# Attention values gathered over half a head from one ring of transposed probabilities

## The chip, the cores and the metric

The kernel runs on one core of one Trainium2 chip. The metric is the device time of one execution in microseconds (us); the time of a kernel is the median over its runs. TensorE (PE) multiplies matrices, VectorE (DVE), ScalarE (ACT) and GpSimd (POOL) do the elementwise work, and SyncE (SP) issues most DMAs. Each engine takes its instructions in a fixed order.

## What is computed

One block of a diffusion model: neighbourhood attention and a convolutional feed-forward network, each with a normalisation, a modulation and a residual. Cut to what matters here:

```python
SEQ, D_MODEL, NA_HEADS, CTX_LEN = 1024, 1024, 16, 256      # head dimension 64
q, k = rms_norm(split_heads(h @ w_q), q_gain), rms_norm(split_heads(h @ w_k), k_gain)
v = split_heads(h @ w_v)                                   # kc, vc: the same of the 256 context rows
# of each query: a window of 8 x 16 keys of the 16 x 64 grid, and all 256 context keys
s = jnp.concatenate([s_loc, s_ctx], axis=-1)
p = jax.nn.softmax(s.astype(jnp.float32), axis=-1)
y = (p_loc @ v_win + p_ctx @ v_ctx) @ w_o                  # per head, then all heads together
x = x + g1 * y
x = x + g2 * conv_ffn(modulate(rms_norm(x, norm2), sh2, sc2))
```

## The kernel before

**Numbers.** Everything is fp32, but most matmuls are done in the faster float32r type on operands split in two: a high half (a ScalarE copy that rounds) and a low half (the rest, a subtraction on VectorE or GpSimd). A product is then two or three matmuls into one PSUM bank.

**Layout.** The 1024 queries are reordered by grid column into NB = 8 blocks of P = 128, so that a query block t needs the key blocks t-1, t and t+1 only (two at the ends) and the two context blocks, which are numbered 8 and 9. There are 16 heads in 8 pairs.

**The attention stage.** A list `steps` goes over pair p, head h and query block t, 128 steps in all (the last head in the order `LORD` = 0, 1, 4, 5, 2, 3, 6, 7). A loop over `si` (lines 576 to 600) issues for each step, in this order:

- `stage_b` of step si: the scores, four matmuls into the PSUM tile `s`; VectorE adds the bias and takes the row's minimum (L412), ScalarE the exponential with its sum (L414), GpSimd divides by the sum (L419). The result is the tile `p`, one of four buffers.
- `stage_a` for the next step, if that begins a pair of query blocks: transposes and splits q.
- 6 fillers.
- `stage_c` of step si-2: TensorE transposes p, block by block, into PSUM (`pl` for the local blocks, `pc` for the context blocks of two steps, L431 and L436); ScalarE copies the high halves (L438, and L441 for the context of two steps) and VectorE the low halves (L439, L442) into `th` and `tl`.
- 5 fillers.
- `stage_d` of step si-3, if that ends a pair of query blocks: gathers the values.
- 5 fillers, and one or two pieces of `mod_gen` (a part of w_mod is loaded, scaled and summed).

A filler is one matmul of other work: the q, k, v projection of the next pair of heads (`qkv_gen`, lines 296 to 351, with `k_stack`), or at the end the output projection of the first eight heads (`wo_first`). The source order gives priorities only: the program's planner (`schedule_with_timeline_sim`) sets the order on each engine by a simulated timeline, and may put ready work of a later place ahead.

**The gather before.** `stage_d` works on two query blocks, 256 columns. The buffers `th` and `tl` hold six key blocks by two query blocks: the four key blocks 2u-1 to 2u+2, and the context. Of the outer local blocks only one query block needs the key block; the other half holds zeros, written once in `make_pt`. For each key block the values v (high half beside low half, as the stationary operand) meet `th` and then `tl` (L450, L451), and all go into the PSUM tile `po`, of which there is one. ScalarE copies one half of the partitions out (L456), VectorE adds the other half (L457), and SyncE stores the sum to `o_dram` (L458). Two pairs of `th` and `tl` alternate (`useq_`).

**PSUM.** Of the eight banks `s` has two, `tr` three (all transposes), `pq` two (projections), `po` one.

**The start.** Before the attention stage, `load_x` and `load_m` put the ten x tiles and three pieces of w_mod in the four buffers of tag `pt`, which `th` and `tl` use afterwards.

Of the kernel before, what the change touches and what calls it, by code (L numbers as in the profile page):

```python
# [10 lines left out]
F32 = mybir.dt.float32  # L11
F32R = mybir.dt.float32r
AF = mybir.ActivationFunctionType
ALU = mybir.AluOpType
# [4 lines left out]
P = 128  # L19
D = 1024  # L20
# [4 lines left out]
NB = 8  # L25
WH, WW = 8, 16
HEADS = 16
DH = 64
# [6 lines left out]
TORD = [NB, NB + 1] + list(range(NB))  # L35
BIG = 1e30
HALF = 512
# [24 lines left out]
def block_kernel(ctx, tc, x, ctxt, cc, w_mod, b_col, b_row, n1, n2, w_qkv, gains, rpb_t, mask_i, mask_r, w_o,  # L62
                 w_up, conv_w, conv_b, w_down, comb, out):
    nc = tc.nc
    PE, ACT, DVE, POOL, SP = nc.tensor, nc.scalar, nc.vector, nc.gpsimd, nc.sync
# [11 lines left out]
    def f(ap):  # L77
        return ap.bitcast(F32)
# [7 lines left out]
    ident = const.tile([P, P], F32, name="ident")  # L86
# [77 lines left out]

    xin = {}

    def load_x(t):
        xt = sa.tile([P, D], F32, tag="pt", bufs=4, name=f"xt{t}")
        if t < NB:
            SP.dma_start(out=xt, in_=xv[t])  # L170
        else:
            SP.dma_start(out=xt, in_=ctxt[(t - NB) * P:(t - NB + 1) * P, :])
        xin[t] = xt
# [25 lines left out]
    with pool("sm") as sm:  # L199
# [5 lines left out]
        def load_m(i):  # L205
            si, k2 = divmod(i, 4)
            if i in PTM:
                mraw[i] = sa.tile([P, 2, HALF], F32, tag="pt", bufs=4, name=f"mraw{i}")
            else:
                mraw[i] = sm.tile([P, 2, HALF], F32, tag="mraw", bufs=MB, name=f"mraw{i}")  # L210
            SP.dma_start(out=mraw[i], in_=wm[:, 2 * k2:2 * k2 + 2, segs[si]:segs[si] + HALF])
# [67 lines left out]
    SP.dma_start(out=mr, in_=mask_r)  # L279
    bias = sb.tile([P, 5, 2 * P], F32, name="bias")  # L280
    POOL.memset(bias[:, 0, :], 0.0)
    pth, ptl = [], []

    def make_pt():
        for i in range(2):
            for l in (pth, ptl):
                l.append(sa.tile([P, 6, 2, P], F32R, tag="pt", bufs=4, name=f"pt{i}_{len(ptl)}"))
                POOL.memset(f(l[i][:, 0, 1, :]), 0.0)
                POOL.memset(f(l[i][:, 3, 0, :]), 0.0)


    qd, kst, vt = {}, {}, {}
    kn = {}
    kdone = set()
# [125 lines left out]
        pn[p, h, t] = w  # L420

    def stage_c(p, h, t):
        u, i = t // 2, t % 2
        lo, hi = max(t - 1, 0), min(t + 2, NB)
        nb = hi - lo
        b0 = lo - (2 * u - 1)
        w = pn.pop((p, h, t))
        th, tl = pth[useq_[p, h, u]], ptl[useq_[p, h, u]]
        pl = ps.tile([P, 3, P], F32, tag="tr", bufs=3, name=f"pl{p}_{h}_{t}")
        for j in range(nb):  # L430
            PE.transpose(pl[:, j, :], w[:, CTX + j * P:CTX + (j + 1) * P], ident)  # L431
        if i == 0:
            ctr[0] = ps.tile([P, 2, 2, P], F32, tag="tr", bufs=3, name=f"pc{p}_{h}_{u}")
        pc = ctr[0]
        for j in range(2):
            PE.transpose(pc[:, j, i, :], w[:, j * P:(j + 1) * P], ident)  # L436
        dh, dl = th[:, b0:b0 + nb, i, :], tl[:, b0:b0 + nb, i, :]
        ACT.activation(dh, pl[:, :nb, :], AF.Copy)  # L438
        DVE.tensor_tensor(dl, pl[:, :nb, :], f(dh), ALU.subtract)  # L439
        if i == 1:  # L440
            ACT.activation(th[:, 4:6], pc, AF.Copy)  # L441
            DVE.tensor_tensor(tl[:, 4:6], pc, f(th[:, 4:6]), ALU.subtract)  # L442

    def stage_d(p, h, u):
        th, tl = pth[useq_[p, h, u]], ptl[useq_[p, h, u]]
        po = ps.tile([P, 2 * P], F32, tag="po", bufs=1, name=f"po{p}_{h}_{u}")
        blks = [(j, 2 * u - 1 + j) for j in range(4) if 0 <= 2 * u - 1 + j < NB] + [(4, NB), (5, NB + 1)]
        for m, (j, kb) in enumerate(blks):
            v = vt[p, h, kb].rearrange("p a b -> p (a b)")
            PE.matmul(po, v, th[:, j].rearrange("p a b -> p (a b)"), start=(m == 0), stop=False)  # L450
            PE.matmul(po, v, tl[:, j].rearrange("p a b -> p (a b)"), start=False, stop=(m == len(blks) - 1))  # L451
        a, b = h * DH, (h + 1) * DH
        o = DH - a
        tmp = sb.tile([P, 2 * P], F32, tag="ot", bufs=1, name=f"ot{p}_{h}_{u}")
        res = sb.tile([P, 2 * P], F32, tag="or", bufs=2, name=f"or{p}_{h}_{u}")
        ACT.activation(tmp[a:b], po[o:o + DH], AF.Copy)  # L456
        DVE.tensor_tensor(res[a:b], po[a:b], tmp[a:b], ALU.add)  # L457
        SP.dma_start(out=o_dram[p, a:b, u * 2 * P:(u + 1) * 2 * P], in_=res[a:b])  # L458


    def mod_gen():
# [79 lines left out]

    steps = [(p, h, t) for p in range(NPAIR) for h in range(2) for t in range(NB)]
    steps[-NB:] = [(NPAIR - 1, 1, t) for t in LORD]
    useq_ = {}
    for p, h, t in steps:
        useq_.setdefault((p, h, t // 2), len(useq_) % 2)
    mg = mod_gen()
    fill = qkv_gen(0)
    stats_x(TORD[2])
    for i, t in enumerate(TORD):  # L550
# [5 lines left out]
        if i >= AHEAD:  # L556
            while (0, 1, TORD[i - AHEAD]) not in vt:
                next(fill)
    make_pt()
# [16 lines left out]
    for si in range(ns + 4):  # L576
# [9 lines left out]
        if si + 1 < ns and steps[si + 1][2] % 2 == 0:  # L586
            p, h, t = steps[si + 1]
            need(p, h, t)
            stage_a(p, h, t // 2)
        filler(6)  # L590
        if 0 <= si - 2 < ns:
            stage_c(*steps[si - 2])
        filler(5)
        if 0 <= si - 3 < ns and steps[si - 3][2] % 2 == 1:
            p, h, t = steps[si - 3]
            stage_d(p, h, t // 2)
        filler(5)
        next(mg, None)
        if si % 4:
# [418 lines left out]
```

## Time and profile before

| | |
|---|---|
| median of 3 runs | 1447.32 us (1444.68 to 1451.52) |
| the profiled execution | 1445.83 us, span 1443.8 us |
| TensorE busy | 1359.0 us, 94% |
| VectorE busy | 1116.8 us, 77% |
| GpSimd busy | 877.8 us, 61% |
| ScalarE busy | 792.3 us, 55% |
| gather matmuls (L450, L451) | 2 x 352, first at 123.0 us, last at 728.8 us |

The span runs from the first to the last instruction. A row such as "L450 PE MATMUL po<-pt,v 128x256 x352 | 93.9, 290 | 3.0" names the line, engine, operation, the tiles written and read, the shape and the count; then busy us, mean ns of one, and the idle time of the engine ahead of them with what ended it. Matmuls are pipelined and their ends are modelled: one of 0.28 us may be followed by the next after 0.12 us. In rows of a stretch each engine has its busy us and, in brackets, its instructions; the last three numbers are the granted TensorE clock, the DMA share and GB/s. Rows in order of time begin with the start and the duration; in brackets at their end stand the idle time ahead and what ended it.

### The profile page before, as it was taken

To read this page: it belongs to the slowest core of one execution; us is meant where nothing else is said; L and a number is where in the kernel's file an instruction comes from. 1 tells how busy PE (TensorE), PEld (TensorE's weight loads), DVE (VectorE), ACT (ScalarE), POOL (GpSimd) and SP (SyncE) were. 2 spreads that over 40 slices of the span, in tenths; PEclk is the share of its full clock that TensorE was granted. 3 is DMA by queue.
4 is the path that set the end of the run, shared out by engine and by line. 5 is a ranking of instruction groups with operands and counts; after the bars stand their busy time and mean duration, and the time that the engine had idled before them with its cause. 6 is when DMAs were issued, how large, how long until landed. Compare 5 with 4: busy or idle time off the path is not lost. (4 is left out here: it accounts for less than half of the span.)

```text
span 1443.8 us, 22131 instructions
## 1 busy us (share of the span) xinstructions
PE 1359.0 (94%) x7396; PEld 1191.2 (83%) x7396; DVE 1116.8 (77%) x2219; ACT 792.3 (55%) x1745; POOL 877.8 (61%) x799
## 2 busy tenths in 40 slices
PE   6699999999999999998996999999999999899998
PEld 2699999999989999987784778888888887678876
DVE  6677777777777778866579978888888886896787
ACT  6776767777776656653466534434444445554421
POOL 1656677767776647745358655555555555667586
PEclk9899999999999999999998999999999999999999
DMA  9612232223131202262143233333223334744345
GB/s 318 170 39 65 61 91 73 90 59 97 58 96 53 70 13 82 64 145 84 36 122 107 81 103 110 110 109 105 94 101 109 110 111 162 251 141 146 115 108 99
DMA packets 84825, 150.12 MB, mean 104 GB/s; under 512 B 9944, under 2 KB 49000, under 8 KB 84712
## 3 DMA queue, kind: packets, MB, share of 16 engines
q1 hardware_dynamic: 82984, 145.57, 32.0%
q0 software_dynamic: 1728, 3.15, 1.5%
q8 instruction: 58, 0.95, 0.3%
q14 instruction: 55, 0.45, 0.1%
HBM read 115.91 MB, written 32.78 MB: 103 GB/s over the span
## 5 line engine op out<-in xcount | busy, mean ns | idle before, releaser
L695 POOL TENSOR_TENSOR u<-ur,u 128x512 fp32r<-128x512 f32 x154 | 232.7, 1527 | 178.7 <-ACT u L692 173.2
L303 PE MATMUL pq<-wh,hth 128*128 128x384 f32 (+1 forms) x640 | 218.5, 341 | 13.5 <-DVE kn L342 10.2
L307 PE MATMUL pq<-wh,htl 128*128 128x384 f32 (+1 forms) x640 | 213.7, 334 | 2.1 <-DVE htl L196 1.2
L419 POOL TENSOR_TENSOR p<-p,m 128x640 f32<-128x640 f32 (+1 forms) x128 | 154.5, 1208 | 98.8 <-DVE m L415 77.3
L305 PE MATMUL pq<-wl,hth 128*128 128x384 f32 (+1 forms) x640 | 212.9, 333 | 0.5 <-POOL wl L149 0.5
L692 ACT ACTIVATE u<-ur 128x512 fp32r<-128x512 f32 x154 | 94.1, 630 | 113.2 <-PE sw L747 42.7
L303 PEld LDWEIGHTS pq<-wh,hth 128*128 128x128 f32 x640 | 123.0, 192 | 17.2 <-DVE kn L342 6.4
L307 PEld LDWEIGHTS pq<-wh,htl 128*128 128x128 f32 x640 | 122.6, 192 | 2.9 <-DVE htl L196 2.9
L794 DVE SCALAR_TENSOR_TENSOR y<-g,cw,y 128x896 f32<-128x896 f32 (+1 forms) x132 | 105.4, 861 | 25.2 <-ACT y L788 25.0
L414 ACT ACTIVATE p<-p,m 128x640 f32<-128x640 f32 (+1 forms) x128 | 102.7, 803 | 39.6 <-DVE m L412 38.2
L305 PEld LDWEIGHTS pq<-wl,hth 128*128 128x128 f32 x640 | 122.8, 192 | 0.7 <-POOL wl L149 0.7
L472 POOL TENSOR_TENSOR macc<-mr,macc 128x256 f32<-128x256 f32 x112 | 84.6, 755 | 42.6 <-ACT mr L470 32.4
L327 POOL TENSOR_TENSOR qss<-qss,mhalf 128x4 f32<-128x4 f32 (+1 forms) x80 | 77.8, 973 | 50.2 <-DVE qss L326 41.4
L450 PE MATMUL po<-pt,v 128*128 128x256 f32 x352 | 93.9, 290 | 3.0 <-DVE m L412 1.7
L877 POOL TENSOR_TENSOR da<-da 128x512 fp32r<-128x512 f32 x44 | 71.9, 1680 | 36.6 <-ACT da L876 36.4
L451 PE MATMUL po<-pt,v 128*128 128x256 f32 x352 | 92.2, 290 | 0.4 <-DVE pt L439 0.4
L903 ACT ACTIVATE db<-dr 128x512 fp32r<-128x512 f32 x77 | 47.0, 626 | 76.5 <-PE dx L922 44.4
L412 DVE CUSTOM_DVE_ANT_0 p<-s,bias 128x640 f32<-128x640 f32 x96 | 78.3, 816 | 10.9 <-PE s L401 10.5
L470 ACT ACTIVATE mr<-mr,cs 128x256 f32<-128x256 f32 x112 | 57.0, 509 | 51.0 <-DMA mr<-in_w_mod_dram 47.9
L904 POOL TENSOR_TENSOR db<-dr,db 128x512 fp32r<-128x512 f32 x44 | 67.2, 1565 | 22.8 <-ACT db L903 22.8
L438 ACT ACTIVATE pt<-pl 128x384 fp32r<-128x384 f32 (+1 forms) x128 | 58.0, 459 | 36.9 <-PE pl L431 36.1
L439 DVE TENSOR_TENSOR pt<-pl,pt 128x384 fp32r<-128x384 f32 (+1 forms) x128 | 65.9, 517 | 15.5 <-ACT pt L438 15.0
(273 smaller groups left out, 4199.7 us busy)
## 6 DMA issues: line engine op xcount, KB each, us to landing
ur<-in_w_up_dram SPq DMA_DIRECT2D x44, 512.0 KB
da<-act_dram SPq DMA_DIRECT2D x77, 256.0 KB
mr<-in_w_mod_dram SPq DMA_DIRECT2D x128, 128.0 KB
dr<-in_w_down_dram SPq DMA_DIRECT2D x22, 512.0 KB
wraw<-in_w_qkv_dram SPq DMA_DIRECT2D x56, 192.0 KB
mraw<-in_w_mod_dram SPq DMA_DIRECT2D x16, 512.0 KB
act_dram<-sa SPq DMA_DIRECT2D x11, 512.0 KB
act_dram<-y SPq DMA_DIRECT2D x11, 512.0 KB
```

The costliest lines, as they stand in the source:

```text
L303: PE.matmul(pq[:, c0:], hth[t][:, k, :], wh[:, c0:], start=(k == 0), stop=False)
L305: PE.matmul(pq[:, c0:], hth[t][:, k, :], wl[:, c0:], start=False, stop=False)
L307: PE.matmul(pq[:, c0:], htl[t][:, k, :], wh[:, c0:], start=False, stop=(k == KC - 1))
L412: DVE.tensor_tensor_reduce(out=dst, in0=src, in1=bb, scale=1.0, scalar=3e38, op0=ALU.add, op1=ALU.min, accum_out=m[:, 0:1])
L414: ACT.activation(w[:, :n], w[:, :n], AF.Exp, bias=m[:, 0:1], scale=-1.0, accum_out=m[:, 1:2])
L419: POOL.tensor_tensor(w[:, :n], w[:, :n], m[:, 2:3].broadcast_to([P, n]), ALU.mult)
L450: PE.matmul(po, v, th[:, j].rearrange("p a b -> p (a b)"), start=(m == 0), stop=False)
L451: PE.matmul(po, v, tl[:, j].rearrange("p a b -> p (a b)"), start=False, stop=(m == len(blks) - 1))
L472: POOL.tensor_tensor(acc, raw, acc, ALU.add)
L692: ACT.activation(s[:, 0], r[op], AF.Copy)
L695: POOL.tensor_tensor(s[:, 1], r[op], f(s[:, 0]), ALU.subtract)
L794: DVE.scalar_tensor_tensor(o, i, w, o, ALU.mult, ALU.add)
```

## The change

The gather is done over four query blocks (512 columns, a full bank) instead of two, but for the last head, which stays with two. `th` and `tl` become one pair of buffers, a ring of four slots, one for each step (`place_`), with five blocks to a slot: up to three local ones, in the order t-1, t, t+1, and two of the context. A matmul of a local key block takes only the one to three query blocks that need it, as a strided operand, and writes only their columns of `po`. The key blocks come in descending order and the context last. `stage_d` is issued ahead of `stage_c` in a step, as the next group's first `stage_c` writes slot 0 again. The zero fills go. The x tiles and three w_mod pieces use the ring's two buffers in four places. The diff, without the lines about names and blank ones:

```diff
+    ring = []
+    early = [sa.tile([P, 4, 5, P], F32, tag="ring", bufs=2, name=f"early{i}") for i in range(2)]
+    def make_ring():
+        ring.extend(sa.tile([P, 4, 5, P], F32R, tag="ring", bufs=2, name=f"ring{i}") for i in range(2))
+    def place(n, shape=(P, D)):
+        a = early[n // 2 % 2].rearrange("p a b n -> p (a b n)")[:, n % 2 * D:(n % 2 + 1) * D]
+        return a if len(shape) == 2 else a.rearrange("p (a b) -> p a b", b=shape[2])
     def load_x(t):
-        xt = sa.tile([P, D], F32, tag="pt", bufs=4, name=f"xt{t}")
+        xt = place(TORD.index(t))
...
-                mraw[i] = sa.tile([P, 2, HALF], F32, tag="pt", bufs=4, name=f"mraw{i}")
+                mraw[i] = place(1 + i - PTM[0], (P, 2, HALF))
...
-    def make_pt():
-        for i in range(2):
-            for l in (pth, ptl):
-                l.append(sa.tile([P, 6, 2, P], F32R, tag="pt", bufs=4, name=f"pt{i}_{len(ptl)}"))
-                POOL.memset(f(l[i][:, 0, 1, :]), 0.0)
-                POOL.memset(f(l[i][:, 3, 0, :]), 0.0)
...
     def stage_c(p, h, t):
-        u, i = t // 2, t % 2
         lo, hi = max(t - 1, 0), min(t + 2, NB)
-        nb = hi - lo
-        b0 = lo - (2 * u - 1)
+        nb, b0, sl = hi - lo, lo - t + 1, place_[p, h, t]
...
-        th, tl = pth[useq_[p, h, u]], ptl[useq_[p, h, u]]
+        th, tl = ring
...
-            PE.transpose(pc[:, j, i, :], w[:, j * P:(j + 1) * P], ident)
-        dh, dl = th[:, b0:b0 + nb, i, :], tl[:, b0:b0 + nb, i, :]
+            PE.transpose(pc[:, sl % 2, j, :], w[:, j * P:(j + 1) * P], ident)
+        dh, dl = th[:, sl, b0:b0 + nb, :], tl[:, sl, b0:b0 + nb, :]
         ACT.activation(dh, pl[:, :nb, :], AF.Copy)
         DVE.tensor_tensor(dl, pl[:, :nb, :], f(dh), ALU.subtract)
-        if i == 1:
-            ACT.activation(th[:, 4:6], pc, AF.Copy)
-            DVE.tensor_tensor(tl[:, 4:6], pc, f(th[:, 4:6]), ALU.subtract)
+        if sl % 2:
+            ch, cl = th[:, sl - 1:sl + 1, 3:, :], tl[:, sl - 1:sl + 1, 3:, :]
+            ACT.activation(ch, pc, AF.Copy)
+            DVE.tensor_tensor(cl, pc, f(ch), ALU.subtract)
-    def stage_d(p, h, u):
-        th, tl = pth[useq_[p, h, u]], ptl[useq_[p, h, u]]
-        po = ps.tile([P, 2 * P], F32, tag="po", bufs=1, name=f"po{p}_{h}_{u}")
-        blks = [(j, 2 * u - 1 + j) for j in range(4) if 0 <= 2 * u - 1 + j < NB] + [(4, NB), (5, NB + 1)]
-        for m, (j, kb) in enumerate(blks):
+    def stage_d(p, h, ts):
+        n0, n = ts[0], len(ts)
+        s0 = place_[p, h, n0]
+        po = ps.tile([P, 4 * P], F32, tag="po", bufs=1, name=f"po{p}_{h}_{n0}")
+        ops = [(kb, max(kb - 1, n0) - n0, min(kb + 2, n0 + n) - n0, kb)
+               for kb in reversed(range(max(n0 - 1, 0), min(n0 + n + 1, NB)))]
+        ops += [(kb, 0, n, None) for kb in (NB, NB + 1)]
+        for m, (kb, a, b, local) in enumerate(ops):
             v = vt[p, h, kb].rearrange("p a b -> p (a b)")
-            PE.matmul(po, v, th[:, j].rearrange("p a b -> p (a b)"), start=(m == 0), stop=False)
-            PE.matmul(po, v, tl[:, j].rearrange("p a b -> p (a b)"), start=False, stop=(m == len(blks) - 1))
+            for i, t5 in enumerate(ring):
+                if local is None:
+                    r = t5[:, s0 + a:s0 + b, 3 + kb - NB, :]
+                else:
+                    o = (s0 + a) * 5 * P + (kb - (n0 + a) + 1) * P
+                    r = t5.rearrange("p a b n -> p (a b n)")
+                    if b - a == 1:
+                        r = r[:, o:o + P]
+                    else:
+                        r = r[:, o:o + (b - a) * 4 * P].rearrange("p (a n) -> p a n", n=4 * P)[:, :, :P]
+                PE.matmul(po[:, a * P:b * P], v, r, start=(m == 0 and i == 0), stop=(m == len(ops) - 1 and i == 1),
+                          skip_group_check=True)
...
-        tmp = sb.tile([P, 2 * P], F32, tag="ot", bufs=1, name=f"ot{p}_{h}_{u}")
-        res = sb.tile([P, 2 * P], F32, tag="or", bufs=2, name=f"or{p}_{h}_{u}")
+        tmp = sb.tile([P, 4 * P], F32, tag="ot", bufs=1, name=f"ot{p}_{h}_{n0}")
+        res = sb.tile([P, 4 * P], F32, tag="or", bufs=2, name=f"or{p}_{h}_{n0}")
...
-        SP.dma_start(out=o_dram[p, a:b, u * 2 * P:(u + 1) * 2 * P], in_=res[a:b])
+        SP.dma_start(out=o_dram[p, a:b, n0 * P:(n0 + n) * P], in_=res[a:b, c])
...
+    place_ = {x: i % 4 for i, x in enumerate(steps)}
+    group = {}
+    for i, x in enumerate(steps):
+        n = 2 if i >= len(steps) - NB else 4
+        if i % n == n - 1:
+            group[x] = [y[2] for y in steps[i + 1 - n:i + 1]]
...
         filler(6)
+        if 0 <= si - 3 < ns and steps[si - 3] in group:
+            p, h, t = steps[si - 3]
+            stage_d(p, h, group[p, h, t])
+        filler(5)
         if 0 <= si - 2 < ns:
             stage_c(*steps[si - 2])
-        filler(5)
-        if 0 <= si - 3 < ns and steps[si - 3][2] % 2 == 1:
-            p, h, t = steps[si - 3]
-            stage_d(p, h, t // 2)
         filler(5)
```

More of the change, by code (lines that the diff above doesn't have):

```diff
@@ L281, in block_kernel @@
     POOL.memset(bias[:, 0, :], 0.0)
-    pth, ptl = [], []
-    def make_pt():
-        for i in range(2):
-            for l in (pth, ptl):
-                l.append(sa.tile([P, 6, 2, P], F32R, tag="pt", bufs=4, name=f"pt{i}_{len(ptl)}"))
-                POOL.memset(f(l[i][:, 0, 1, :]), 0.0)
-                POOL.memset(f(l[i][:, 3, 0, :]), 0.0)
     qd, kst, vt = {}, {}, {}
@@ L431, in stage_c @@
             PE.transpose(pl[:, j, :], w[:, CTX + j * P:CTX + (j + 1) * P], ident)
-        if i == 0:
-            ctr[0] = ps.tile([P, 2, 2, P], F32, tag="tr", bufs=3, name=f"pc{p}_{h}_{u}")
+        if sl % 2 == 0:
+            ctr[0] = ps.tile([P, 2, 2, P], F32, tag="tr", bufs=3, name=f"pc{p}_{h}_{t}")
         pc = ctr[0]
         for j in range(2):
-            PE.transpose(pc[:, j, i, :], w[:, j * P:(j + 1) * P], ident)
-        dh, dl = th[:, b0:b0 + nb, i, :], tl[:, b0:b0 + nb, i, :]
+            PE.transpose(pc[:, sl % 2, j, :], w[:, j * P:(j + 1) * P], ident)
@@ L452, in stage_d @@
         a, b = h * DH, (h + 1) * DH
         o = DH - a
-        tmp = sb.tile([P, 2 * P], F32, tag="ot", bufs=1, name=f"ot{p}_{h}_{u}")
-        res = sb.tile([P, 2 * P], F32, tag="or", bufs=2, name=f"or{p}_{h}_{u}")
-        ACT.activation(tmp[a:b], po[o:o + DH], AF.Copy)
-        DVE.tensor_tensor(res[a:b], po[a:b], tmp[a:b], ALU.add)
-        SP.dma_start(out=o_dram[p, a:b, u * 2 * P:(u + 1) * 2 * P], in_=res[a:b])
+        tmp = sb.tile([P, 4 * P], F32, tag="ot", bufs=1, name=f"ot{p}_{h}_{n0}")
@@ L461, in mod_gen @@
+        res = sb.tile([P, 4 * P], F32, tag="or", bufs=2, name=f"or{p}_{h}_{n0}")
+        c = slice(0, n * P)
+        ACT.activation(tmp[a:b, c], po[o:o + DH, c], AF.Copy)
+        DVE.tensor_tensor(res[a:b, c], po[a:b, c], tmp[a:b, c], ALU.add)
+        SP.dma_start(out=o_dram[p, a:b, n0 * P:(n0 + n) * P], in_=res[a:b, c])
     def mod_gen():
@@ L543, in block_kernel @@
     steps[-NB:] = [(NPAIR - 1, 1, t) for t in LORD]
-    useq_ = {}
-    for p, h, t in steps:
-        useq_.setdefault((p, h, t // 2), len(useq_) % 2)
+    place_ = {x: i % 4 for i, x in enumerate(steps)}
[4 more added lines that the diff above has]
+            group[x] = [y[2] for y in steps[i + 1 - n:i + 1]]
     mg = mod_gen()
@@ L558, in block_kernel @@
                 next(fill)
-    make_pt()
+    make_ring()
     def filler(n):
```

## The prediction

> **What bounds the kernel now.** I read the page's busy shares first, then the busy time by stretch, then TensorE's own waits, then the order of time. All numbers are of one profiled execution of 1445.83 us with a span of 1443.8 us.
>
> ```profile
> span 1443.8 us, 22131 instructions
> PE 1359.0 (94%) x7396; PEld 1191.2 (83%) x7396; DVE 1116.8 (77%) x2219; ACT 792.3 (55%) x1745; POOL 877.8 (61%) x799
> 110.00:640.00 530.00, 515.31 (x3533) 499.31 (x3533) 406.34 (x1220) 369.08 (x966) 359.53 (x396) 1.00 0.24 71
> 1000.00:1100.00 100.00, 100.00 (x443) 82.81 (x442) 81.89 (x103) 43.67 (x65) 54.00 (x37) 1.00 0.27 93
> ```
>
> The change lies in the attention stage, 110 to about 730 us. In 110 to 640 us TensorE is busy 515 of 530 us at a granted clock of 1.00, VectorE 406, ScalarE 369, GpSimd 360. A TensorE that is busy 97% could still be padded, so I ask what it waits for.
>
> ```profile
> PE py L526 <- DVE x L529: 5.3, 1, 5.3
> PE pq L303 <- DVE kn L342: 4.8, 7, 1.1
> PE s L400 <- ACT qh L389: 2.1, 4, 1.2
> PE s L400 <- DVE m L412: 2.0, 4, 0.8
> PE po L450 <- DVE m L412: 1.7, 1, 1.7
> ...
> PE po L450 <- ACT pt L438: 0.8, 2, 0.4
> PE po L450 <- DVE or L457: 0.5, 1, 0.5
> ...
> PE po L451 <- DVE pt L439: 0.4, 1, 0.4
> ...
> PE py L528 <- POOL ohl L520: 0.2, 1, 0.2
> ```
>
> These are its waits from 110 to 730 us (total, times, longest); the fifteen rows of that view, the last one shown at the end, add to 22 us. So the stage is TensorE's, and a matmul taken out there is worth nearly its own time, as long as no new wait comes. The waits on the gather's operands and its bank (the four po rows) are 3.4 us together, over 64 gathers.
>
> **What one matmul costs.** The modelled durations overlap, so I use start to start.
>
> ```profile
> L450 PE MATMUL po<-pt,v 128*128 128x256 f32 x352 | 93.9, 290 | 3.0 <-DVE m L412 1.7 <-ACT pt L438 0.8 <-DVE or L457 0.5
> L451 PE MATMUL po<-pt,v 128*128 128x256 f32 x352 | 92.2, 290 | 0.4 <-DVE pt L439 0.4
> 269.19 0.28 PE L450 MATMUL po<-pt,v 128*128 128x256 f32 x1
> ...
> 270.03 0.28 PE L451 MATMUL po<-pt,v 128*128 128x256 f32 x1
> 270.15 0.34 PE L303 MATMUL pq<-wh,hth 128*128 128x384 f32 x1
> ...
> 270.85 0.34 PE L305 MATMUL pq<-wl,hth 128*128 128x384 f32 x1
> L431 PE MATMUL pl<-ident,p 128*128 128x128 f32 x352 | 58.0, 273 | 1.1 <-POOL p L419 1.1
> 531.07 0.49 PE L431 MATMUL pl<-ident,p 128*128 128x128 f32 x3
> ```
>
> - 256 columns: from 269.19 to 270.15 eight gather matmuls start: 0.96/8 = 0.120 us (0.119 over a longer stretch; I take 0.119).
> - 384 columns: 270.15 to 270.85, four steps: 0.175.
> - 512 columns: the window 1000 to 1100 holds 443 of them back to back: 0.226.
> - 128 columns: three transposes take 0.49 us in all, one alone 0.273, so (0.49 - 0.273)/2 = 0.109. There the weight load, which is always 128 columns, probably sets the pace. The gather has no 128-column row; 0.111 is my value, between 0.06 (scaling the 256-column row down) and 0.119 (the 256-column row itself).
>
> **Part 1, the gather (stage_d).** Before, a quarter head of two query blocks has 5 or 6 key blocks (5 at the ends of the sequence), each with two matmuls of 256 columns, half of some being zeros. A half head is 5 + 6 = 11 blocks, 22 matmuls: 22 x 0.119 = 2.62 us. Thirty-two half heads make the 704 of the two rows. After, a half head in the steady form has two context blocks of 512 columns and five local ones of 1, 2, 3, 3 and 2 query blocks, each twice: 4 x 0.226 + 4 x 0.175 + 4 x 0.119 + 2 x 0.111 = 0.904 + 0.700 + 0.476 + 0.222 = 2.30 us, 14 matmuls. That saves 0.32 us in each of 30 half heads: 9.6 us. The last head keeps groups of two blocks: the same number of matmuls, twelve of them narrower at 0.008 each, 0.1 us: nothing. With 128 columns at 0.06 the saving is 0.42 a half head, 12.7 us; at 0.119 it is 9.1.
>
> The local operands are now read in runs of 128 elements with a stride, the context in four runs. Every moving operand in the trace is one run. If a run costs nothing, 9.6 stands. The upper bound comes from the fixed part of a matmul: 0.119 at 256 and 0.226 at 512 columns leave 0.119 - (0.226 - 0.119) = 0.012 us that doesn't scale; if each extra run cost that much, 24 extra runs in a half head are 0.29 us and eat 8.6 us. I take nothing, because the runs are long and the columns set the slope.
>
> The Trainium skill, "TensorE: Matmul & The Clock Gate", section Back-to-back issue gap, gives a sustained pace of 131 ns for 512 columns and 81 ns for 128. By that the new half head would be an estimated 1.86 us and the gain about 23 us. The window of 443 matmuls at 0.226 us contradicts it, with the clock at 1.00, so the sum goes by the row.
>
> **Part 2, the copies out.** The bank is now evicted 34 times instead of 64.
>
> ```profile
> L456 ACT ACTIVATE ot<-po x64: 375/379/384, 124.9 to 729.4; 64x256 f32<-64x256 f32 x64
> L457 DVE TENSOR_TENSOR or<-po,ot x64: 395/422/430, 126.3 to 729.8; 64x256 f32<-64x256 f32 x64
> L441 ACT ACTIVATE pt<-pc x64: 577/592/612, 117.4 to 723.8; 128x512 fp32r<-128x512 f32 x64
> L442 DVE TENSOR_TENSOR pt<-pc,pt x64: 669/685/693, 118.1 to 724.4; 128x512 fp32r<-128x512 f32 x64
> L458 SPq DMA_DIRECT2D o_dram<-or x64: 445/452/912, 126.7 to 730.3; - x64
> L288 POOL MEMSET pt<- x4: 204/204/204, 81.8 to 97.3; 128x128 f32 x4
> ```
>
> A 512-wide one of the same kind takes 0.592 and 0.685 us. ScalarE: 64 x 0.379 = 24.3 to 30 x 0.592 + 4 x 0.379 = 19.3, 5 us less; VectorE: 64 x 0.422 = 27.0 to 30 x 0.685 + 4 x 0.422 = 22.2, 5 us less. Neither bounds the stage, so 0 on the path; from below, they may come sooner to what TensorE waits for (2 us of gain). SyncE issues 30 fewer stores of 0.45 us; it still holds the next w_mod, weight and bias loads behind each store that waits for its sum, but half as often: 0. The eight zero fills (four at each of two lines, 0.204 each, 1.6 us of GpSimd before 98 us) go; GpSimd is not the bound: 0. The one bank is full now and its eviction, 0.59 + 0.69 us, lies in the four steps to the next gather: 0.
>
> **Part 3, the order and the single ring.** The probabilities of four steps now share one pair of buffers, where two pairs alternated. So stage_d must have read slot 0 before the next stage_c writes it, and stage_d is moved ahead of stage_c and five fillers. The new dependence is a loop: the last transposes of a group, their copies on ScalarE and VectorE, the gather, then the first copy of the next group. In source order the old gather had 21 fillers, the scores and a stage_c between itself and the transposes it needs: 21 x 0.175 + 2 x 0.175 + 2 x 0.119 + 5 x 0.109 = 4.8 us. The new one has 11 fillers and the scores: 1.93 + 0.59 = 2.5 us. What must fit in there:
>
> ```profile
> 263.47 0.49 PE L431 MATMUL pl<-ident,p 128*128 128x128 f32 x3
> 267.04 0.47 ACT L438 ACTIVATE pt<-pl 128x384 fp32r<-128x384 f32 x1
> 267.54 0.56 DVE L439 TENSOR_TENSOR pt<-pl,pt 128x384 fp32r<-128x384 f32 x1 [0.99 <-ACT pt L438]
> ...
> 531.59 0.49 ACT L438 ACTIVATE pt<-pl 128x384 fp32r<-128x384 f32 x1 [2.61 <-PE pl L431]
> 532.12 0.56 DVE L439 TENSOR_TENSOR pt<-pl,pt 128x384 fp32r<-128x384 f32 x1
> ```
>
> The second case, whose transposes are the x3 row at 531.07, is the prompt one: the third starts at 531.29, the low half is done at 532.68, 1.4 us later, and the gather waits for nothing. The first is a late one: 263.69 to 268.10, 4.4 us, because ScalarE was held up; a gather 2.5 us behind would stand for 1.9 us. So the wait of a gather lies between 0 and 1.9 us. The context is gathered last, 10 matmuls or 1.4 us after the first, so its copies, the last of a step, don't decide. The order on each engine is the planner's and not the source's (it puts other ready work ahead of a gather that it believes late), which is why the 64 gathers of before cost only 3.4 us in waits, 0.05 each. With half the slack I take 0.13 each, nearer to that row than to the late case: 34 x 0.13 = 4.4, that is 1.0 us more than before.
>
> stage_c itself comes 2.3 + 0.9 us later in every fourth step, 0.9 in the others. It waits for GpSimd's division; a later place can only shorten those waits (1.1 us in the L431 row). It holds its buffer p longer, one of four, where the 620 us hold 128 steps of 4.8 us: nothing.
>
> **Part 4, the start.** The x tiles and three w_mod pieces take four 4 KB places in two 10 KB tiles in place of four tiles, each used in the same turn: 0. Should a wait be kept for a whole 10 KB tile, the transposes of one x tile would wait for the load into its neighbour.
>
> ```profile
> L184 PE MATMUL pt<-ident,xt 128*128 128x128 f32 x80 | 11.9, 296 | 4.4 <-DVE xt L178 4.4
>   DMA xt<-in_x_dram: 3.9, 4
> ```
>
> Today's loads cost 3.9 us of idle time in four waits, about 1 us each; five more are 5 us at most.
>
> **The sum.** -9.6 (gather) + 1.0 (waits ahead of it) + 0 = -8.6 us: 1445.83 - 8.6 = 1437.2 for an execution like the profiled one. The median of the three runs, 1447.32, lies 1.5 us above that execution, so I say 1438.7.
>
> **Rivals.** One number decides between the first three: the mean wait w ahead of a gather. The change gives -9.6 - 3.4 + 34 w.
>
> - *The gain is eaten* (w about 0.38): 1447.3. For it: the slack is halved, and ScalarE is late at times. Against: 1.4 us is the prompt chain, and in every fourth step only.
> - *Slower: the ring closes a loop.* A gather that comes late holds slot 0, so the next group's copy waits in ScalarE's queue with scores, exponentials and qkv copies behind it, and its PSUM bank is one of three that the transposes share. This decides from w = (7.2 + 13.0)/34 = 0.59 us; with 0.8 us it is +14.2: 1461.5. For it: the 4.4 us case above. Against: 0.59 us on average needs a late case in every third group, and 64 gathers wait 3.4 us in all now.
> - *More than the gather*: ScalarE's and VectorE's 5 us less each also take a third of the stage's 22 us of waits: 1431.
> - *Strided runs cost* 0.012 us each: 1447.3.
> - *Wide matmuls stream faster than 0.226 us* next to their weight loads, 0.13 for the four of a half head (about what the 256-column row shows): 11.5 us more, 1427. Against it stands the window of 443. The pace named in the Trainium skill above is this rival.
>
> **Chances.** 0.5% (7.2 us) is about what a measurement of this kernel can tell from no change; so faster means under 1440.1, slower over 1454.6. Forecast 0.48, own range 1434 to 1443, of which 0.40 is under 1440.1 and 0.08 in the band; more than the gather 0.12; wide matmuls 0.02; eaten 0.22; strided runs 0.04; slower 0.12. Faster 0.40 + 0.12 + 0.02 = 0.54, same 0.08 + 0.22 + 0.04 = 0.34, slower 0.12. The range goes from the case below, less 1 us, to the band's end with little of the slower case: 1430 to 1453.
>
> **What the changed profile would show.** 30 x 14 + 44 = 464 gather matmuls in place of 704, 512-wide ones 0.226 apart, 128-wide ones 0.11 apart (0.06 or 0.12 mends the first term). Waits of TensorE on the gather's operands of about 4 us in all; if 13 or more, the second rival holds; if ScalarE's copies into the ring wait for TensorE's gather, the third. The last gather, at 728.7 us now, starts at about 720. The stages behind it keep their length. The forecast fails if the planner's new order brings other waits, at pq or s, which no row of before can show.

## The result, and the profile after

The changed kernel takes 1467.43 us (median, 1464.9 to 1470.22) against 1447.98 us in the same comparison: a ratio of 1.0144, 95% interval 1.0119 to 1.0169. It is slower by some 20 us where 9 us of gain were forecast. The profiled execution took 1464.9 us.

The page of the changed kernel (line numbers have moved: the scores are L402 and L403, the projections L305 to L309, the gather is L467), and two stretches: the one that was shown of before, and the whole stage.

```profile
span 1463.1 us, 21522 instructions
PE 1366.9 (93%) x7156; PEld 1181.1 (81%) x7156; DVE 1105.9 (76%) x2189; ACT 784.8 (54%) x1715; POOL 873.2 (60%) x791
110.00:640.00 530.00, 500.47 (x3192) 470.63 (x3193) 381.37 (x1150) 352.61 (x912) 349.56 (x386) 0.98 0.22 66
110.00:745.00 635.00, 598.50 (x3713) 553.73 (x3714) 445.70 (x1293) 398.67 (x1012) 389.39 (x420) 0.98 0.25 71
```

In the same 530 us TensorE did 3192 instructions where it did 3533. The gather has fewer matmuls now and ScalarE and VectorE have fewer copies out, but every engine got through less (VectorE 1150 instead of 1220, GpSimd, whose work in the stage is the same, 386 instead of 396), so the stage runs slower. The groups of the gather, its copies out and their first and last start, from the view of the tile `po` (the counts by shape at the end of its first row are of every third matmul):

```profile
L467 PE MATMUL po<-ring,v x464: 220/337/562, 123.2 to 744.1; 128*128 128x256 f32 x53, 128*128 128x384 f32 x40, 128*128 128x512 f32 x40, 128*128 128x128 f32 x22
L474 ACT ACTIVATE ot<-po x34: 375/592/598, 127.3 to 744.5; 64x512 f32<-64x512 f32 x30, 64x256 f32<-64x256 f32 x4
L475 DVE TENSOR_TENSOR or<-po,ot x34: 427/680/695, 127.9 to 745.6; 64x512 f32<-64x512 f32 x30, 64x256 f32<-64x256 f32 x4
```

464 matmuls and 34 copies out, as forecast. The first gather matmul starts at 123.2 us, as before (123.0 in the table of before is its weight load); the last at 744.1 instead of 728.8, where about 720 was forecast. So 15 of the 19 us between the two profiled executions lie in the attention stage, none in the start. The other 4 lie behind it, in unchanged code; there the stretch from the last gather to the end lies between 714.6 and 725.4 us over all the kernels of this study, in no order that follows the edits, and I build nothing on it.

TensorE's waits in the stage, 110 to 745 us (the first rows, and those on the gather):

```profile
PE pq L305 <- DVE kn L344: 7.0, 10, 1.4
PE s L402 <- DVE ql L392: 4.1, 2, 3.4
PE s L402 <- DVE m L414: 2.9, 4, 1.1
PE s L402 <- ACT qh L391: 2.6, 4, 0.7
PE pl L431 <- DVE ring L443: 2.0, 1, 2.0
PE pc L436 <- POOL p L421: 2.0, 4, 0.7
...
PE po L467 <- DVE ring L439: 1.3, 2, 1.1
...
PE po L467 <- DVE or L475: 1.0, 1, 1.0
...
PE po L467 <- ACT ring L438: 0.5, 2, 0.3
```

The gather itself waits 2.8 us in all, less than before (3.4). The waits have come everywhere else: at the projections, the scores, the transposes. Looking only at what waits *at the changed instruction* would find nothing wrong.

The modelled durations hide short waits, so I also took every matmul's start to the next one's start, from 110 us to the end of the last gather, and split it: its own spacing by width (0.227, 0.174, 0.119 and 0.109 us for 512, 384, 256 and 128 columns), what goes over that by more than 0.2 us ("waits"), and the rest (smaller gaps and matmuls at a lower clock). The sums of all gaps in a trace, which come to about half a us less than the stage, as the first matmul starts a little after 110 us:

| kernel | stage, us | own spacing | waits | rest |
|---|---|---|---|---|
| before | 619.1 | 573.9 | 29.7 | 15.1 |
| changed | 634.4 | 562.1 | 49.5 | 22.3 |
| ascending (e6_asc, below) | 622.1 | 562.9 | 39.6 | 19.1 |

The matmul work fell by 12 us (9.6 were forecast; a few records are missing in each trace, so the difference means little). Waits grew by 20, the rest by 7.

### The profile page after: what moved, and what is told of

Its sections match the earlier page's. It is cut to its first block, busy times and chain, and to the rows that moved or that the text cites. A ratio compares the mean times of both kernels' runs of the same rounds, so it can differ in the third digit from the quotient of the medians.

```text
span 1463.1 us, 21522 instructions
## 1 busy us (share of the span) xinstructions
PE 1366.9 (93%) x7156; PEld 1181.1 (81%) x7156; DVE 1105.9 (76%) x2189; ACT 784.8 (54%) x1715; POOL 873.2 (60%) x791
## 5 line engine op out<-in xcount | busy, mean ns | idle before, releaser
L718 POOL TENSOR_TENSOR u<-ur,u 128x512 fp32r<-128x512 f32 x154 | 228.8, 1498 | 180.0 <-ACT u L715 178.2
L305 PE MATMUL pq<-wh,hth 128*128 128x384 f32 (+1 forms) x640 | 220.3, 344 | 12.9 <-DVE kn L344 7.0
L309 PE MATMUL pq<-wh,htl 128*128 128x384 f32 (+1 forms) x640 | 215.7, 337 | 0.5 <-DVE htl L208 0.5
L305 PEld LDWEIGHTS pq<-wh,hth 128*128 128x128 f32 x640 | 124.9, 195 | 19.4 <-DVE kn L344 11.2
L309 PEld LDWEIGHTS pq<-wh,htl 128*128 128x128 f32 x640 | 124.4, 194 | 1.5 <-DVE htl L208 1.0
L817 DVE SCALAR_TENSOR_TENSOR y<-g,cw,y 128x896 f32<-128x896 f32 (+2 forms) x132 | 98.8, 812 | 23.8 <-ACT y L811 23.3
L414 DVE CUSTOM_DVE_ANT_0 p<-s,bias 128x640 f32<-128x640 f32 x96 | 78.6, 818 | 18.0 <-PE s L403 15.2
L467 PE MATMUL po<-ring,v 128*128 128x256 f32 (+3 forms) x464 | 88.3, 330 | 2.8 <-DVE ring L439 1.3
L439 DVE TENSOR_TENSOR ring<-pl,ring 128x384 fp32r<-128x384 f32 (+1 forms) x128 | 66.2, 518 | 23.2 <-ACT ring L438 22.1
L467 PEld LDWEIGHTS po<-ring,v 128*128 128x128 f32 x464 | 71.0, 189 | 7.9 <-ACT ring L438 2.5
L438 ACT ACTIVATE ring<-pl 128x384 fp32r<-128x384 f32 (+1 forms) x128 | 58.5, 458 | 29.6 <-PE pl L431 25.6
```

The source lines that it names most:

```text
L305: PE.matmul(pq[:, c0:], hth[t][:, k, :], wh[:, c0:], start=(k == 0), stop=False)
L309: PE.matmul(pq[:, c0:], htl[t][:, k, :], wh[:, c0:], start=False, stop=(k == KC - 1))
L467: PE.matmul(po[:, a * P:b * P], v, r, start=(m == 0 and i == 0), stop=(m == len(ops) - 1 and i == 1), skip_group_check=True)
L718: POOL.tensor_tensor(s[:, 1], r[op], f(s[:, 0]), ALU.subtract)
L817: DVE.scalar_tensor_tensor(o, i, w, o, ALU.mult, ALU.add)
```

## The experiments

**Noise and the order of the two stages.** The first runs ask which part costs the time: the place of `stage_d`, the single ring, the size of the gather, or nothing in particular.

e0_null:

```diff
-        filler(6)
+        filler(5)
         if 0 <= si - 2 < ns:
             stage_c(*steps[si - 2])
-        filler(5)
+        filler(6)
```

> The kernel before with one filler moved from ahead of stage_c to behind it (5, 6, 5 instead of 6, 5, 5): no work is changed. Theory 'planner's order' (any small move in the source changes the planner's order and with it the waits, by ten us and more either way): off by 5 to 20 us from before, in either direction. The other theories (a certain part of the change costs the time): within 4 us of before.

Measured 1.0009 of before (0.9987 to 1.0031). This small shift is worth nothing, and the larger one of e1_swap below no more than 0.5%, so the theory "planner's order" (any move costs ten us and more) falls.

e1_swap:

```diff
+        if 0 <= si - 3 < ns and steps[si - 3][2] % 2 == 1:
+            p, h, t = steps[si - 3]
+            stage_d(p, h, t // 2)
+        filler(5)
         if 0 <= si - 2 < ns:
             stage_c(*steps[si - 2])
         filler(5)
-        if 0 <= si - 3 < ns and steps[si - 3][2] % 2 == 1:
-            p, h, t = steps[si - 3]
-            stage_d(p, h, t // 2)
-        filler(5)
```

> The kernel before with its own gather of two query blocks, issued ahead of stage_c as in the changed kernel, and nothing else. Theory 'order' (stage_c comes later in a step, and the gather has half the slack): slower by 15 to 28 us, with most of the 28 us of TensorE waits that the change brought. Theories 'single ring' and 'lump' (below): within 4 us of before. Theory 'planner's order': 5 to 20 us either way.

Measured 0.9974 (0.9953 to 0.9995): if anything faster. The halved slack between transposes and gather, on which the prediction's waits rested, costs nothing. Of the kernels that do all the work it is the only one whose interval lies under 1, by 0.05% to 0.5%.

**The ring and the size.** e4_pairs:

```diff
-        n = 2 if i >= len(steps) - NB else 4
+        n = 2
```

> The changed kernel with groups of two steps in every head: the strided operands without zeros, the ring of four slots, the new order, but gathers of 256 columns, so that the ring holds two groups that alternate. Theory 'single ring' (the first stage_c of a group must wait for the gather, which must wait for the last copies): 0 to 5 us faster than before, as the ring is double. Theory 'lump' (2.3 us of gather in one step of four upsets the engines that feed TensorE): the same, 0 to 5 us faster. Theory 'order': 12 to 25 us slower than before. Planner's order: 5 to 20 us either way.

Measured 1.0104 (1.0081 to 1.0128). With two groups that alternate in the ring and with small gathers most of the loss is there, 15 us of some 20, so neither the single ring nor the lump is the main cause, and the order of the two stages was ruled out above. None of my theories had this.

e5_pairs_cd: the same, and `stage_c` ahead of the gather again:

```diff
+        if 0 <= si - 2 < ns:
+            stage_c(*steps[si - 2])
+        filler(5)
         if 0 <= si - 3 < ns and steps[si - 3] in group:
             p, h, t = steps[si - 3]
             stage_d(p, h, group[p, h, t])
         filler(5)
-        if 0 <= si - 2 < ns:
-            stage_c(*steps[si - 2])
```

> As the kernel with groups of two, but with stage_c ahead of the gather as in the kernel before: only the layout without zeros and the strided operands are left of the change. 'Order', 'single ring' and 'lump' all expect 0 to 5 us faster than before (twelve narrower matmuls in a head, 0.02 to 0.06 us each: 4 to 11 us less TensorE work). A strided operand that costs: slower by 3 to 9 us. Planner's order: 5 to 20 us either way.

Measured 1.0109 (1.0089 to 1.0128), the same as e4_pairs: here too the place of `stage_d` makes no difference. So what costs is in the little that this has left of the change. In its trace no gather starts before the high-half copy of its newest step is done; in that of before, 27 of 64 do, each with two matmuls. Here is one such gather of before, its rows in order of time (high half L450, low half L451, copies L438 and L439; of the two copies in the L438 row the first is this gather's newest), with a row at its end that shows when it closed:

```profile
145.02 0.28 PE L450 MATMUL po<-pt,v 128*128 128x256 f32 x1
145.14 0.28 PE L451 MATMUL po<-pt,v 128*128 128x256 f32 x1
147.36 0.90 ACT L438 ACTIVATE pt<-pl 128x256 fp32r<-128x256 f32 x2
148.03 0.36 PE L450 MATMUL po<-pt,v 128*128 128x256 f32 x1
148.41 0.42 DVE L439 TENSOR_TENSOR pt<-pl,pt 128x256 fp32r<-128x256 f32 x1
149.24 0.28 PE L451 MATMUL po<-pt,v 128*128 128x256 f32 x1
...
150.27 0.38 ACT L456 ACTIVATE ot<-po 64x256 f32<-64x256 f32 x1 [0.25 <-PE po L451]
```

The oldest key block needs only the first of the two steps; its two matmuls go 2.3 us ahead of the newest copy, where TensorE had room. And one of the changed kernel:

```profile
298.24 0.37 ACT L438 ACTIVATE ring<-pl 128x256 fp32r<-128x256 f32 x1
298.86 0.36 PE L467 MATMUL po<-ring,v 128*128 128x256 f32 x1
299.56 0.42 DVE L439 TENSOR_TENSOR ring<-pl,ring 128x256 fp32r<-128x256 f32 x1
300.40 2.39 PE L467 MATMUL po<-ring,v 128*128 128x256 f32 x13
300.71 0.82 DVE L414 CUSTOM_DVE_ANT_0 p<-s,bias 128x640 f32<-128x640 f32 x1 [0.73 <-PE po L467]
```

In descending order the newest key block comes first, and nothing of the gather can go before its copy: one matmul after the high half, and after the low half the other thirteen in one piece of 2.39 us.

**Descending or ascending.** e6_asc:

```diff
-               for kb in reversed(range(max(n0 - 1, 0), min(n0 + n + 1, NB)))]
+               for kb in range(max(n0 - 1, 0), min(n0 + n + 1, NB))]
```

> The changed kernel with its local key blocks in ascending order, context still last; nothing else. Theory 'first operand' (descending order makes a gather begin with the newest step's copy, so it can't be spread over the steps before; of the 64 gathers of before 27 begin ahead of the newest step's copy, of the changed kernel's 34 none): gathers begin early again, the added waits of some 25 us go, and the 9.6 us of matmul time come out: 3 to 12 us faster than before. Theory 'ring tile' (one tile with four slots in place of two tiles, or its strided operands, changes what the planner thinks ready): still 10 to 20 us slower than before.

Measured 1.0011 (0.9989 to 1.0033): the one word gives back all of the loss, but the forecast gain does not appear. 31 of the 34 gathers begin ahead of their newest copy, mostly with four or six matmuls, 149 in all.

e7_pairs_cd_asc, on e5_pairs_cd:

```diff
-               for kb in reversed(range(max(n0 - 1, 0), min(n0 + n + 1, NB)))]
+               for kb in range(max(n0 - 1, 0), min(n0 + n + 1, NB))]
```

> Groups of two, stage_c ahead of the gather, key blocks ascending: of the change only the ring as one tile, the layout without zeros and the strided operands are left. 'First operand': 0 to 6 us faster than before. 'Ring tile': 10 to 16 us slower, as the same kernel in descending order.

Measured 1.0020 (1.0003 to 1.0037), 13 us under its descending twin, far from what "ring tile" expects, but not the gain of "first operand" either. The ring tile and the strided operands cost at most 0.4%, net of the matmul work that the narrower operands save.

e8_before_desc:

```diff
-        blks = [(j, 2 * u - 1 + j) for j in range(4) if 0 <= 2 * u - 1 + j < NB] + [(4, NB), (5, NB + 1)]
+        blks = [(j, 2 * u - 1 + j) for j in reversed(range(4)) if 0 <= 2 * u - 1 + j < NB] + [(4, NB), (5, NB + 1)]
```

> The kernel before with its local key blocks in descending order, context last; nothing else. 'First operand': slower by 8 to 16 us, with no gather that begins ahead of the newest copy. 'Ring tile': within 4 us of before.

Measured 1.0099 (1.0076 to 1.0122), and no gather starts ahead of its newest copy. The word alone, in the old kernel with the old work, brings a loss of 14 us. Its row of the stretch, against before's 515.31 us, 3533 instructions and clock 1.00:

```profile
110.00:640.00 530.00, 505.58 (x3446) 486.98 (x3445) 391.85 (x1187) 362.06 (x946) 352.06 (x391) 0.99 0.22 66
```

e9_before_ctx1:

```diff
-        blks = [(j, 2 * u - 1 + j) for j in range(4) if 0 <= 2 * u - 1 + j < NB] + [(4, NB), (5, NB + 1)]
+        blks = [(4, NB), (5, NB + 1)] + [(j, 2 * u - 1 + j) for j in range(4) if 0 <= 2 * u - 1 + j < NB]
```

> The kernel before with the two context blocks first in the gather and the local blocks ascending behind them. The context copies of both steps are made with the second step, so this too makes a gather begin with the newest copies, by another way. 'First operand': slower by 8 to 16 us. If only the local order matters, or neither does: within 4 us of before.

Measured 1.0050 (1.0032 to 1.0068), just short of what "first operand" expects: 7 us slower. No gather starts before its context's copy, its first operand here, is done. But that copy starts ahead of the newest local one in 51 of the 64 gathers (in 52 of before), and 104 matmuls go ahead of the newest local copy, so the run separates less than I meant it to.

e12_newest_first, with one key block alone moved to the front:

```diff
-        blks = [(j, 2 * u - 1 + j) for j in range(4) if 0 <= 2 * u - 1 + j < NB] + [(4, NB), (5, NB + 1)]
+        blks = [(j, 2 * u - 1 + j) for j in (3, 0, 1, 2) if 0 <= 2 * u - 1 + j < NB] + [(4, NB), (5, NB + 1)]
```

> The kernel before with the key block of the newest step's own first (order 3, 0, 1, 2, then the context; at the end of a sequence there is no block 3 and the order is as before). Theory 'first operand' (the gather can't begin before the newest copy, whatever comes after): as slow as in descending order, 1.005 to 1.012 of before. Theory 'order within' (what matters is how many of the gather's matmuls are ready one after another, and one late block does little): within 4 us of before.

Measured 1.0118 (1.0089 to 1.0146). As slow as fully descending, with the other blocks ascending: what counts is what stands in front. 11 gathers still begin early, at ends of the sequence, where the order is as before.

e15_oldest_then_desc, from the changed kernel:

```diff
+        ops = ops[-1:] + ops[:-1]
         ops += [(kb, 0, n, None) for kb in (NB, NB + 1)]
```

> The changed kernel (descending) with the oldest key block alone put first. Theory 'opening' (only the first operand matters: a gather that has begun can be spread): within 4 us of the ascending kernel, so 0 to 5 us over before. Theory 'fixed order' (the matmuls into one bank keep their order, so all that stand behind the newest operand wait for it; only 2 of 14 can go early): 12 to 19 us slower than before, as the changed kernel.

Measured 1.0082 (1.0052 to 1.0113), about half way between the ascending kernel and the changed one, 12 us slower than before. 32 of 34 gathers now begin early, each with exactly the two matmuls that stand ahead of the newest operand, and about half of the loss is still there, so a bare beginning isn't enough in a gather of 14. Counting in each trace the gather matmuls that start before the newest step's high-half copy is done:

| gather | matmuls ahead of the newest copy | ratio to before |
|---|---|---|
| four steps, descending (changed) | 0 | 1.0144 |
| four steps, oldest, then descending | 64 | 1.0082 |
| four steps, ascending | 149 | 1.0011 |
| two steps, descending (e4, e5, e8) | 0, 0, 0 | 1.0104, 1.0109, 1.0099 |
| two steps, newest first (e12) | 22 | 1.0118 |
| two steps, ascending (e7, e16) | 52, 58 | 1.0020, 1.0026 |
| two steps, context first (e9) | 104 | 1.0050 |

Within each size the loss goes roughly with what can start early; e9, whose first operand is another one, doesn't fit this count. How much one early matmul is worth is not settled: the 54 of before are some 6 us of work, 15 us hang on them, and the planner's own timeline, in which the order is made, is in no trace.

**Where the 9.6 us stay.** e10_before_less (128 matmuls of 256 columns left out):

```diff
-            PE.matmul(po, v, th[:, j].rearrange("p a b -> p (a b)"), start=(m == 0), stop=False)
-            PE.matmul(po, v, tl[:, j].rearrange("p a b -> p (a b)"), start=False, stop=(m == len(blks) - 1))
+            PE.matmul(po, v, th[:, j].rearrange("p a b -> p (a b)"), start=(m == 0), stop=(m == len(blks) - 1))
+            if j < 4:
+                PE.matmul(po, v, tl[:, j].rearrange("p a b -> p (a b)"), start=False, stop=False)
```

> The kernel before without the matmuls of the context's low half (128 of 256 columns, 0.119 us each: 15.2 us of TensorE work); the copies stay. Theory 'TensorE bound' (what is taken out of TensorE in this stage comes off the time, as the prediction had it): 12 to 15 us faster than before. Theory 'loop bound' (the stage keeps the step of the chain scores, minimum, exponential, division, transposes, copies, gather as the planner laid it, and less matmul work turns into waits): 0 to 5 us faster.

Measured 0.9950 (0.9931 to 0.9968): 7 us of 15 (5 to 10). Neither theory's band holds it all. In its trace 16 us less of own spacing meet 11 us more of waits: 557.8 + 40.6 + 16.2 us in a stage of 614.8 us, against 573.9 + 29.7 + 15.1 before.

e11_asc_less:

```diff
-            for i, t5 in enumerate(ring):
+            for i, t5 in enumerate(ring[:1] if local is None else ring):
```

(on e6_asc)

> The changed kernel with ascending key blocks, without the matmuls of the context's low half (64 or so of 512 columns, 0.226 us each: about 15 us of TensorE work); the copies stay. 'TensorE bound': 12 to 15 us faster than the same kernel with them. 'Loop bound': 0 to 5 us faster than it.

Measured 0.9910 (0.9879 to 0.9941), that is some 15 us under e6_asc by the two ratios, with some 5 us of uncertainty: here the matmul time does come off. In its trace own spacing is 14 us lower than e6_asc's, waits 5 higher (548.9 + 44.9 + 19.2). In these two runs TensorE work counts in this stage, at a rate somewhere between a third and one.

e13_asc_late, on e6_asc:

```diff
-        filler(6)
+        filler(11)
         if 0 <= si - 3 < ns and steps[si - 3] in group:
             p, h, t = steps[si - 3]
             stage_d(p, h, group[p, h, t])
-        filler(5)
         if 0 <= si - 2 < ns:
             stage_c(*steps[si - 2])
```

> The changed kernel with ascending key blocks and the gather issued after 11 fillers, just ahead of stage_c, in place of after 6. 'TensorE bound, gather too early in the source' (scores and transposes wait behind gather matmuls that the planner put ahead): 3 to 9 us faster than before. 'Loop bound': within 4 us of the ascending kernel with 6 fillers, 0 to 3 us over before.

Measured 1.0033 (1.0013 to 1.0054), 5 us slower than before, so a later place of the gather doesn't bring the gain. e14_split, on e6_asc:

```diff
         for m, (kb, a, b, local) in enumerate(ops):
+            if part == 0 and kb > n0 or part == 1 and kb <= n0:
+                continue
...
-            stage_d(p, h, group[p, h, t])
+            stage_d(p, h, group[p, h, t], 1 if len(group[p, h, t]) == 4 else 2)
+        if 0 <= si - 3 < ns - NB and (si - 3) % 4 == 1:
+            p, h, t = steps[si - 3]
+            stage_d(p, h, [t - 1, t, t + 1, t + 2], 0)
```

> The changed kernel with ascending key blocks, the gather issued in two parts: the two oldest key blocks when the group's second step is transposed, the rest when its fourth is. Theory 'TensorE bound, priority' (the waits that took the gain come from the planner's late or clumped gather matmuls): 3 to 9 us faster than before. Theory 'loop bound' (less matmul work turns into waits at the scores wherever the gather stands): within 4 us of before.

Measured 1.0029 (1.0006 to 1.0051), 4 us slower where "priority" expects a gain, though its stage, 617.6 us in the profiled execution, is a little shorter than before's. e16_pairs_asc, on e4_pairs:

```diff
-               for kb in reversed(range(max(n0 - 1, 0), min(n0 + n + 1, NB)))]
+               for kb in range(max(n0 - 1, 0), min(n0 + n + 1, NB))]
```

> Groups of two, key blocks ascending, gather ahead of stage_c. If the lost gain comes from the half head's gather (14 matmuls over 13 us in one bank): 2 to 6 us faster than before, as with the old gather in this order. If from the ring tile and its layout: 0 to 5 us slower, as the groups of two with stage_c first.

Measured 1.0026 (1.0004 to 1.0047), 11 us under its descending twin. So the size of the gather doesn't eat the gain; the run comes out as its expectation has it for the ring tile and its layout. All five ascending kernels with the ring, whatever the size and place of the gather, lie between 1.0011 and 1.0033. The matmul work is saved in each (562.9 us of own spacing in e6_asc, e13_asc_late and e14_split) and comes back in the main as waits. The four largest of e6_asc, 110 to 732 us:

```profile
PE s L402 <- DVE m L414: 8.5, 6, 4.9
PE s L402 <- ACT qh L391: 5.1, 6, 1.5
PE qt L388 <- DVE ring L439: 3.7, 2, 3.5
PE po L467 <- ACT ring L438: 1.6, 1, 1.6
```

The scores wait for their one PSUM tile (L414 must have read it) and for the query's split. That these waits fill what the gather leaves is what the sums show; which engine's lag sets them isn't settled. Nor is it whether the ring's layout itself costs what the gather saves: e11_asc_less shows that a kernel with the ring can gain from less matmul work, and no run takes the layout alone. A second ring, which would let `stage_c` go ahead of a half head's gather, was not tried.

## Why the prediction was wrong

The forecast was 1438.7 us and the kernel took 1467.43, 29 us more. Some 19 of these are the descending order, which had no term in the sum (1.0144 against 1.0011 with the order alone turned round); the other 10 are the gain of the gather, which doesn't appear in the ascending kernel either.

**What bounds the kernel: half right.** TensorE was 97% busy with 22 us of waits, and I concluded that a matmul's own time comes off. e10_before_less took out 15 us and gained 5 to 10, and of the 9.6 us that the gather saves none shows in e6_asc. A small sum of waits says how little is lost now, not how much will be lost when the work shrinks: the order on each engine is made anew for every program.

**Part 1, the gather: right in its work.** 464 matmuls; a half head is 14 of them, and from the medians from start to start that follow I estimate 2.31 us for it, forecast 2.30. By width, from 110 to 745 us:

```profile
L467 PE MATMUL po<-ring,v 128*128 128x256 f32 x152 | 34.4, 300 | 1.3 <-DVE ring L439 1.1 <-ACT ring L438 0.2
L467 PE MATMUL po<-ring,v 128*128 128x512 f32 x120 | 33.6, 401 | 0.0
L467 PE MATMUL po<-ring,v 128*128 128x384 f32 x120 | 26.0, 338 | 0.0
L467 PE MATMUL po<-ring,v 128*128 128x128 f32 x72 | 15.3, 260 | 1.5 <-DVE or L475 1.0 <-ACT ring L438 0.3 <-DVE ring L439 0.2
```

The mean durations of strided operands (0.300, 0.338) stand beside 0.290 (L450, before) and 0.33 to 0.34 (single projections) of unbroken ones of the same width: a run of 128 elements costs next to nothing. From start to start the medians inside the gather are 0.122, 0.176 and 0.234 us at 256, 384 and 512 columns, against 0.120, 0.174 and 0.227 of unbroken operands; by these I estimate some 0.05 us for a half head, where the rival "strided runs cost" needs 0.29. That rival falls, and so does the one with wide matmuls at 0.13 us: 512 columns stay at 0.234. The Trainium skill, "TensorE: Matmul & The Clock Gate", Back-to-back issue gap, names 131 ns for them; this trace doesn't agree.

**Part 2, the copies out: right.** 0.592 and 0.680 us, forecast 0.592 and 0.685; TensorE waits 1.0 us in all for the bank (L475).

**Part 3: the step that failed.** It says "With half the slack I take 0.13 each, nearer to that row than to the late case". The waits at the gather came to 2.8/34 = 0.08 us each, so the row was read rightly, and e1_swap shows that the slack was not the matter at all. (It also calls the context's copies the last of a step, but before they start ahead of the newest local copy in 52 of 64 gathers. Nothing in the sum hangs on it.) What failed is the sentence beside it, that the planner "puts other ready work ahead of a gather that it believes late". I took this for a protection without a price. Before, in 27 of 64 gathers, two of the gather's own matmuls were such ready work and filled TensorE while the newest copies were made. In descending order the newest operand comes first, and none of the gather's matmuls can be such work any more. Part 3 lets the gather begin with the newest copies without asking whether it did so before, and the order got no term of the sum: it was put at nothing without a reason, and the runs put it at 14 us in the old kernel (e8_before_desc) and some 19 in the new one (e6_asc). What the planner then puts ahead are, as I read it, projections, and they are missing afterwards. One place in the changed kernel, TensorE alone:

```profile
256.72 0.33 PE L309 MATMUL pq<-wh,htl 128*128 128x384 f32 x1
...
258.50 2.38 PE L467 MATMUL po<-ring,v 128*128 128x256 f32 x13
260.72 0.38 PE L436 MATMUL pc<-ident,p 128*128 128x128 f32 x2
...
262.89 0.44 PE L388 MATMUL qt<-ident,q 128*128 128x128 f32 x2 [0.77 <-DVE ring L439]
264.02 0.53 PE L402 MATMUL s<-k,qh 128*128 128x384 f32 x1 [0.70 <-ACT qh L391]
...
265.52 0.88 PE L431 MATMUL pl<-ident,p 128*128 128x128 f32 x3 [0.75 <-DVE k L366]
266.19 0.63 PE L436 MATMUL pc<-ident,p 128*128 128x128 f32 x2
266.81 0.58 PE L305 MATMUL pq<-wh,hth 128*128 128x256 f32 x1
...
269.75 0.41 PE L307 MATMUL pq<-wl,hth 128*128 128x256 f32 x1
269.96 0.41 PE L309 MATMUL pq<-wh,htl 128*128 128x256 f32 x1
```

The last projection goes at 256.72; a solid 2.38 us of gather follows, and then scores and transposes only, several of which wait for VectorE or ScalarE, until the projections go on at 266.81. Such stretches of over 5 us without a projection number 2 in the stage of before (10 us in all), 15 here (120 us), 8 in e8_before_desc (58 us), but also 10 in e6_asc (61 us), so they don't measure the loss. ScalarE's largest change among the waits of 110 to 640 us is at the square (L326, `qsq`) that follows a projection (before, then changed):

```profile
ACT qsq L324 <- PE pq L307: 12.9, 13, 1.7
```

```profile
ACT qsq L326 <- PE pq L309: 36.9, 23, 4.3
```

Its queue stands at a projection that TensorE hasn't finished, and what is queued behind it is late for TensorE. This is not how the loss spreads in general: the same wait is 15.8 us in e8_before_desc, 15.2 in e12_newest_first and 5.5 in e4_pairs, which are slow as well. That the order of the gather's operands brings the loss is shown, in both directions; by which chain it spreads stays open.

**Part 4, the start: right**, 0 (the first gather matmul at 123.2 us in both).

**The rivals.** "Slower: the ring closes a loop" gave 1461.5 us, near the 1467.43, but by a mechanism that isn't there: e4_pairs has a ring whose two groups alternate and still loses 15 us, and ScalarE's copies wait for the gather for 3.1 us in all. "The gain is eaten" is what happens to the ascending kernel, though not by w, the wait ahead of the gather. The last line, that other waits come "at pq or s, which no row of before can show", named two of the places where they came (7 us at pq and 12 at s, of 36; before, 5 and 4 of 22), without a chance of its own.

## What to carry to other kernels

In these traces the matmuls of an accumulation run in the order in which they are written (e15_oldest_then_desc: the two ahead of the newest operand go early, none of those behind it), so the operand that is ready last belongs at the end: what stands behind it can't fill the time until it comes. When a change reorders an accumulation, ask for each matmul when its operand is ready, not only what it costs, and look in the trace whether the group now starts before its newest operand. The waits that a wrong order brings need not appear at the reordered instructions (2.8 us there in the changed kernel, though 10.8 in e12_newest_first), so count the instructions that all engines get through in a stretch before looking for the place.

## What the runs showed of the hardware

TensorE's granted clock fell in a stretch with many waits, and so their cost can be more than themselves. The ten us with the waits above, and the ten before them:

```profile
250.00:260.00 10.00, 8.87 (x55) 8.26 (x56) 8.47 (x21) 9.32 (x25) 8.08 (x10) 1.00 0.38 113
260.00:270.00 10.00, 7.59 (x34) 5.90 (x33) 8.96 (x26) 6.05 (x17) 7.11 (x7) 0.71 0.41 125
```

TensorE was busy 7.6 of 10 us, and the clock was 0.71. More closely, it was busy 1.74 of 3.40 us from 260.8 to 264.2, at a clock of 1.00, and then 6.15 of 6.90 us from 264.2 to 271.1, at 0.51. The Trainium skill, "TensorE: Matmul & The Clock Gate", Part 1, puts the fall to half the clock after an idle window of about 3.4 us. The trace agrees that thin stretches lose the clock, but here it fell with no idle gap above 0.77 us in the view, so several short ones seem to do it too. In the rows above a 256-column projection then starts 0.21 us after the one before it (269.75, 269.96), where the full clock gives 0.119. Over 110 to 640 us the mean was 1.00 before, 0.98 in the changed kernel and 0.98 in the ascending one, which has fewer waits, so the mean doesn't follow the waits closely.

Narrow matmuls came cheaper in pairs than the 0.111 us that I took: two of 128 columns with the same values start 0.06 us apart, though each has its own weight load, so the load doesn't set their pace, as the prediction thought it probably did. The next one follows after 0.11 us where it has 512 columns and after 0.14 us in half of the cases where it has 256.
